# Two transformer blocks in split fp32 on one core: GpSimd makes no weights' low parts after the attention in the latent mixers

## The chip, the core and the metric

One core of a Trainium2 chip. The time is the device time of one execution in microseconds, median of the runs. TensorE (PE) multiplies; the vector engine (DVE), ScalarE (ACT) and GpSimd (POOL) work beside it, each through its own list of instructions in order; SyncE (SP) issues the transfers.

## What is computed

The program runs two blocks one after the other; the change lies in the first, which has two layers. Each layer mixes 512 latent tokens (and, in layer 0, 256 context tokens) of width 1024. The mixer, cut to what matters here:

```
def merge_branches(z, attn_o, ...):
    conv_o = conformer_conv(z[..., V_END:CONV_END], ...)   # depthwise conv of 31 taps, layer norm, silu, 1024x1024 product
    pool_o = multiscale_pool(z[..., CONV_END:POOL_END], pool_w, pool_scale)
    gates = jax.nn.sigmoid(z[..., POOL_END:].reshape(z.shape[:-1] + (N_BRANCH, D_MODEL)))
    m = gates[..., 0, :] * attn_o + gates[..., 1, :] * conv_o + gates[..., 2, :] * pool_o
    return m @ w_out + b_out
```

with z = h @ w_in + b_in, everything in float32.

## The kernel before

A product in float32 is made from three matmuls of halves (L181 to L183): each operand is kept as a high part (a rounded copy) and a low part (the value minus the high part). Weights come in units of 1024 rows by 128 columns (512 KB). `Net.unit` fetches one into one of three `raw` buffers (SyncE, L167), ScalarE casts the high part (L152), and then the low part is made (L153, `tensor_sub`), on the vector engine or on GpSimd. A counter decides:

```
on_pool = self.units * self.pool_share % 12 < self.pool_share
```

For the whole mixer `pool_share` is 6 in the latent streams, so that every second unit's low part is GpSimd's; before the mixer and behind its pointwise product it is 0. A `raw` buffer is free for the next fetch when its low part is made.

A latent mixer runs in this order. First the attention, between whose steps the first channel blocks of the depthwise convolution are started. Then `rest()`: what is left of the convolution's products, the pooling branch, and the gates of attention (`gate0`, `between`) and pooling. Then `conv_ln`, woven with the convolution's gate (`gate1`); then `pointwise`; then the output product.

Who does what there:
- the convolution: eight channel blocks, each a chain of 30 taps on the vector engine (L830, one instruction per tap of 128x512). `chain_work` releases taps between the other steps.
- the pooling branch (`pooled`): L902 copies a product into `pad` (ScalarE); L914 adds shifted copies, L918 multiplies, L919 subtracts (GpSimd); the result is cast (ScalarE, L152) and its low part made (vector engine, L153). `mixed` multiplies it (L936, L937 on the vector engine).
- `gate0`: L877 (ScalarE), L882 (GpSimd), L883 (vector engine), eight times.
- `conv_ln`: L964 transposes the eight blocks on TensorE for their moments, a matmul each spreads mean and scale over the partitions (R[0] and R[1], L977 and L979); then per block L983 (GpSimd), L984 (vector engine), L986 and L987 (ScalarE), L988 (vector engine) and a split.
- layer 0 also carries, as `extra`, the products that make the next modulation vectors (L499 to L509): they take units of another weight, L504 copies the row on ScalarE and L506 multiplies it.

A tiling framework schedules the instructions, so the order on each engine follows from its own estimates and isn't that of the text. PSUM has three buffers for products, named mm.

Of the kernel before, what the change touches and what calls it, by code (L numbers as in the profile page):

```python
# [1679 lines left out]
def run(*gens):  # L1680
    for g in gens:
        for _ in g:
            pass


def weave(*gens):

    live = [list(g) for g in gens]
    while live:
        for e in list(live):  # L1690
            e.append(0) if len(e) == 2 else None
            e[2] += e[1]
            while e[2] >= 1:
                e[2] -= 1
                if next(e[0], "end") == "end":
                    live.remove(e)
                    break


def first_block(net, stop=None):  # L1700
    nc, A = net.nc, net.A
    lat, cx = Stream("lat", 0, LAT), Stream("ctx", 1, CTX)
# [5 lines left out]
    def chain_work(chains, n):  # L1708

        if net.mark is None:  # L1710
            return
        with net.tc.issue_after(net.mark.ins):
            while n > 0 and chains:
                for c in list(chains[:2]):
                    if next(c, "end") == "end":
                        chains.remove(c)
                    n -= 1

    def mix(l, S, X, kT, vs, nkeys, rope, bc_mod, xin, xout, h_out, before_out=None, extra=None):

        od = net.dram([P, KD, S.T])
        m = net.chunked(S.T)
        convh = net.chunked(S.T)
        chains, chains2 = [], []
        conv = net.conv_gemm(l, S, X, convh, chains, chains2)
        with net.tc.issue_after(net.mark.ins) if net.mark else nullcontext():
            for _ in range(FRONT[S.nt]):
                next(conv)

        def gap():  # L1730
            for _ in range(GAP[S.nt]):
                if len(chains) < net.BUFS["pad"]:
                    with net.tc.issue_after(net.pe_mark.ins):
                        next(conv, None)

        def attn():
            for kv in range(2):
                qt = {}

                def dst(t, qt=qt):  # L1740
                    if t // 2 not in qt:
                        qt[t // 2] = net.sb([P, 2, 2, 4, P], F32R, "s8")
                    return qt[t // 2][:, t % 2]

                yield from net.q_half(l, X, kv, rope, dst)
                yield from net.attend(S.nt, dst, kT[kv], lambda kc, kv=kv: vs(kc, kv), nkeys,
                                      lambda t, h, kv=kv: od[:, 4 * kv + h : 4 * kv + h + 2, t * P : t * P + P],
                                      lambda t, h, kv=kv: sums[:, t, 4 * kv + h : 4 * kv + h + 1], gap)

        n = 0  # L1750
        net.mark = net.pe_mark = None
        sums = net.sb([P, S.nt, 8], F32, "sums")
        net.pool_share = SHARE[S.nt]
        for _ in attn():
            n += 1
            chain_work(chains, RATE[S.nt])
            chain_work(chains2, 5)
            if extra is not None and n % EXTRA[S.nt] == 0:
                next(extra, None)
        sig = net.chunked(S.T)  # L1760
        rows = net.inverse_rows(sums, S.nt)
        bout = net.bias_rows([A["b_out"][l, 512 * i : 512 * i + 512] for i in range(2)], 2.0)

        def rest():
            yield from conv
            yield from net.pool_branch(l, S, X, m, net.gate0(l, S, X, m, od, lambda: rows))

        for n, _ in enumerate(rest()):
            chain_work(chains, 10)
            chain_work(chains2, 3)  # L1770
            if extra is not None and n % REXT[S.nt][0] == REXT[S.nt][1]:
                next(extra, None)
        if extra is not None:
            run(extra)
        chain_work(chains, 1000)
        chain_work(chains2, 1000)
        C = Feat(net, S.T, KD)
        if X.full is not None:
            C.full = convh
        weave((net.conv_ln(l, S, convh, C), 1.5), (net.gate1(l, S, X, sig), 1))  # L1780
        M = Feat(net, S.T, KD)
        bc = net.ln_prep(A["ln1_g"][l], A["ln1_b"][l], bc_mod, net.gate_row(l, S.s, 0))
        run(net.pointwise(l, S, C, sig, m, M))
        net.pool_share = 0
        if before_out is not None:
            before_out()
        run(net.out_ln(S, M, A["w_out"][l], bout, bc, xin, xout, h_out))
# [60 lines left out]
    with net.tc.issue_after(net.pe_mark.ins):  # L1848
        net.load_cols(0)
    Xl = []  # L1850
    mix(0, cx, Xc, kT, lambda kc, kv: V(kc)[:, kv * P : kv * P + P], CTX, False,
        None, c0, xd["ctx", 0], None,
        before_out=lambda: Xl.append(net.first_h(lat, x0, 0)), extra=net.ada(0, 4, 6))
# [4 lines left out]
    Xcf = []  # L1858
    Xf = Feat(net, LAT, KD)
    mix(0, lat, Xl, kT, vs, LAT + CTX, True, net.mod_rows(0, 0, 1), x0, xd["lat", 0], h_feat(Xf),  # L1860
        before_out=lambda: Xcf.append(reload(cx, xd["ctx", 0], net.mod_rows(0, 1, 1))), extra=net.ada(0, 6, 12))
    if stop == "mix0":
# [12 lines left out]
    vs = lat_keys(1, X1, kT, V, Xc1)  # L1875
    Xf = Feat(net, LAT, KD)
    mix(1, lat, X1, kT, vs, LAT + CTX, True, net.mod_rows(1, 0, 1), xd["lat", 1], xd["lat", 2], h_feat(Xf))
    if stop == "mix1":
        return xd["lat", 2], None
# [112 lines left out]
```

## Time and profile before

| | us |
|---|---|
| median of 3 runs | 3969.94 (3968.89 to 3973.01) |
| profiled execution | 3973.06 |
| its span, first to last instruction | 3971.3 |
| TensorE busy | 3743.3 (94%), mean granted clock 0.973 |
| vector engine busy | 2541.1 (64%) |
| ScalarE busy | 1438.2 (36%) |
| GpSimd busy | 904.4 (23%) |

Busy times are sums over the span. In square brackets behind an instruction of a timeline stands how long its engine was idle before it, and which instruction released it. A tile's name is its tag; the number behind it, where one is given, says which tile of that tag it is.

### The profile page before, as it was taken

To read this page: it belongs to the slowest core of one execution; us is meant where nothing else is said; L and a number is where in the kernel's file an instruction comes from. 1 tells how busy PE (TensorE), PEld (TensorE's weight loads), DVE (VectorE), ACT (ScalarE), POOL (GpSimd) and SP (SyncE) were. 2 spreads that over 40 slices of the span, in tenths; PEclk is the share of its full clock that TensorE was granted. 3 is DMA by queue.
4 is the path that set the end of the run, shared out by engine and by line. 5 is a ranking of instruction groups with operands and counts; after the bars stand their busy time and mean duration, and the time that the engine had idled before them with its cause. 6 is when DMAs were issued, how large, how long until landed. Compare 5 with 4: busy or idle time off the path is not lost. (4 is left out here: it accounts for less than half of the span.)

```text
span 3971.3 us, 48183 instructions
## 1 busy us (share of the span) xinstructions
PE 3743.3 (94%) x18265; PEld 3098.8 (78%) x18265; DVE 2541.1 (64%) x3600; ACT 1438.2 (36%) x2608; POOL 904.4 (23%) x978
## 2 busy tenths in 40 slices
PE   7899998799899999899989899999899999999999
PEld 3688886577688888688767788889788888778887
DVE  2987888967876656878886645563454346764444
ACT  1535443334222222344324233234432235643223
POOL 0441423673200002522554200110000002420000
PEclk8999999899899999899999999999999999999999
DMA  5567223454343333222333423333233332033332
GB/s 189 144 166 220 88 63 90 118 150 156 110 143 117 123 117 103 79 72 62 103 96 120 132 85 117 106 123 99 84 98 95 97 102 65 17 96 96 96 101 90
DMA packets 491474, 429.49 MB, mean 108 GB/s; under 512 B 29590, under 2 KB 389630, under 8 KB 491242
## 3 DMA queue, kind: packets, MB, share of 16 engines
q1 hardware_dynamic: 491162, 426.16, 35.2%
q8 instruction: 143, 2.34, 0.2%
q14 instruction: 89, 0.73, 0.1%
q0 software_dynamic: 80, 0.26, 0.0%
HBM read 404.70 MB, written 21.65 MB: 107 GB/s over the span
## 5 line engine op out<-in xcount | busy, mean ns | idle before, releaser
L181 PE MATMUL mm<-s,w 128*128 128x512 f32 (+2 forms) x2840 | 1044.3, 370 | 37.1 <-ACT t L877 9.5
L182 PE MATMUL mm<-s,w 128*128 128x512 f32 (+2 forms) x2840 | 1040.8, 367 | 13.5 <-DVE s L153 13.5
L183 PE MATMUL mm<-s,w 128*128 128x512 f32 (+2 forms) x2840 | 1037.7, 366 | 0.0
L152 ACT CAST w<-raw 128x1024 fp32r<-128x1024 f32 (+3 forms) x570 | 582.4, 1026 | 769.7 <-PE mm L183 429.6
L153 DVE TENSOR_TENSOR w<-raw,w 128x1024 fp32r<-128x1024 f32 (+3 forms) x484 | 628.8, 1302 | 273.4 <-ACT w L152 268.3
L181 PE MATMUL mm<-w,s 128*128 128x512 f32 (+2 forms) x1928 | 735.8, 382 | 8.9 <-DVE t L1098 3.7
L182 PE MATMUL mm<-w,s 128*128 128x512 f32 (+2 forms) x1928 | 728.2, 378 | 1.3 <-DVE w L153 1.3
L183 PE MATMUL mm<-w,s 128*128 128x512 f32 (+2 forms) x1928 | 726.6, 379 | 0.8 <-DVE s L153 0.8
L181 PEld LDWEIGHTS mm<-s,w 128*128 128x128 f32 (+1 forms) x2840 | 539.2, 191 | 137.5 <-ACT t L877 10.3
L182 PEld LDWEIGHTS mm<-s,w 128*128 128x128 f32 (+1 forms) x2840 | 541.2, 191 | 100.5 <-DVE s L153 16.3
L183 PEld LDWEIGHTS mm<-s,w 128*128 128x128 f32 (+1 forms) x2840 | 540.6, 190 | 86.5 <-issue 0.2
L830 DVE SCALAR_TENSOR_TENSOR s<-pad,cols,s 128x512 f32<-128x512 f32 (+1 forms) x690 | 523.4, 811 | 1.7
L181 PEld LDWEIGHTS mm<-w,s 128*128 128x128 f32 x1928 | 364.2, 189 | 85.0 <-issue 7.3
L182 PEld LDWEIGHTS mm<-w,s 128*128 128x128 f32 x1928 | 364.3, 189 | 64.4 <-DVE w L153 2.2
L183 PEld LDWEIGHTS mm<-w,s 128*128 128x128 f32 x1928 | 363.9, 189 | 63.8 <-DVE s L153 1.6
L360 POOL TENSOR_SCALAR st<-st 128x1 f32<-128x1 f32 (+2 forms) x91 | 32.2, 354 | 1269.3 <-ACT s L1217 900.2
L153 POOL TENSOR_TENSOR w<-raw,w 128x1024 fp32r<-128x1024 f32 (+1 forms) x86 | 244.2, 2842 | 286.3 <-ACT w L152 276.0
L152 ACT CAST s<-b 128x256 fp32r<-128x256 f32 (+2 forms) x224 | 104.5, 474 | 176.6 <-DVE s L153 90.6
L1232 DVE TENSOR_TENSOR s<-s,mm 128x512 f32<-128x512 f32 x80 | 54.6, 685 | 172.0 <-PE mm L183 172.0
L1054 POOL MEMSET pad<- 128x1 f32 x66 | 6.4, 99 | 650.0 <-DVE t L1061 648.8
L153 DVE TENSOR_TENSOR s<-b,s 128x256 fp32r<-128x256 f32 (+2 forms) x224 | 119.7, 545 | 43.8 <-ACT s L152 42.6
L1248 DVE TENSOR_TENSOR t<-t 128x512 f32<-128x512 f32 x64 | 44.2, 691 | 153.3 <-ACT t L1247 153.3
(297 smaller groups left out, 4423.8 us busy)
## 6 DMA issues: line engine op xcount, KB each, us to landing
raw<-in_w_up SPq DMA_DIRECT2D x152, 512.0 KB
raw<-in_w_in SPq DMA_DIRECT2D x147, 512.0 KB
raw<-in_w_down SPq DMA_DIRECT2D x108, 512.0 KB
w<-in_w_ada SPq DMA_DIRECT2D x48, 512.0 KB
w<-in_w_in SPq DMA_DIRECT2D x33, 512.0 KB
raw<-in_w_ada SPq DMA_DIRECT2D x32, 512.0 KB
raw<-in_w_out SPq DMA_DIRECT2D x24, 512.0 KB
t<-d SPq DMA_DIRECT2D x44, 256.0 KB
```

Source lines behind the costliest of these rows:

```text
L152: self.nc.scalar.copy(hi, src)
L153: (eng or self.nc.vector).tensor_sub(lo, src, hi.bitcast(F32))
L181: mm(out, lhsT=l[0], rhs=r[0], start=first, stop=False)
L182: mm(out, lhsT=l[0], rhs=r[1], start=False, stop=False)
L183: return mm(out, lhsT=l[1], rhs=r[0], start=False, stop=last)
L360: nc.gpsimd.tensor_scalar(out, src, scalar1=scale, scalar2=eps, op0=ALU.mult, op1=ALU.add)
L830: nc.vector.scalar_tensor_tensor(out=o, in0=pad[:, k : k + T], scalar=self.col("dww", 8 * k + j), in1=o, op0=ALU.mult, op1=ALU.add)
L1054: nc.gpsimd.memset(pad[:, 0:1], 0.0)
L1232: nc.vector.tensor_add(x(t)[:, cs], x(t)[:, cs], ps)
L1248: nc.vector.tensor_mul(r, r, r)
```

## The change

The counter is set to 0 for the latent streams as soon as the attention loop has ended, not only behind the pointwise product:

```
@@ -1757,6 +1757,8 @@
             chain_work(chains2, 5)
             if extra is not None and n % EXTRA[S.nt] == 0:
                 next(extra, None)
+        if S is lat:
+            net.pool_share = 0
         sig = net.chunked(S.T)
         rows = net.inverse_rows(sums, S.nt)
         bout = net.bias_rows([A["b_out"][l, 512 * i : 512 * i + 512] for i in range(2)], 2.0)
```

56 low parts go from GpSimd to the vector engine, 34 in layer 0 and 22 in layer 1; 52 are of 128x1024, four of 128x512. GpSimd's low parts in the context mixer, in the attentions and in the second block stay. The scheduler orders the engines' lists anew around it.

On the vector engine in layer 0, w_5974 and w_5979 are units of the modulation product mm_5982, w_6009 is the pooling weight; s_862 are the convolution's blocks 4 to 7, whose taps read pad_4702, pad_4891 and pad_5081. Before:

```order
L153 TENSOR_TENSOR w_5974<-raw_5972,w_5974 128x1024
L153 TENSOR_TENSOR s_972_5685<-pad_5736,s_972_5685 128x512
L830 SCALAR_TENSOR_TENSOR s_862_5043<-pad_5081,cols_301,s_862_5043 128x512
L830 SCALAR_TENSOR_TENSOR s_862_5043<-pad_4891,cols_301,s_862_5043 128x512
L830 SCALAR_TENSOR_TENSOR s_862_5043<-pad_5081,cols_301,s_862_5043 128x512
L883 SCALAR_TENSOR_TENSOR s_996_5833<-t_1000_5875,s_1001_5877 128x512
L830 SCALAR_TENSOR_TENSOR s_862_5043<-pad_4891,cols_301,s_862_5043 128x512
L830 SCALAR_TENSOR_TENSOR s_862_5043<-pad_5081,cols_301,s_862_5043 128x512
L830 SCALAR_TENSOR_TENSOR s_862_5043<-pad_4891,cols_301,s_862_5043 128x512
```

and the list of the change at the same place:

```order
L153 TENSOR_TENSOR s_972_5685<-pad_5736,s_972_5685 128x512
L830 SCALAR_TENSOR_TENSOR s_862_5043<-pad_4702,cols_301,s_862_5043 128x512
L153 TENSOR_TENSOR w_5974<-raw_5972,w_5974 128x1024
L830 SCALAR_TENSOR_TENSOR s_862_5043<-pad_5081,cols_301,s_862_5043 128x512
L830 SCALAR_TENSOR_TENSOR s_862_5043<-pad_4891,cols_301,s_862_5043 128x512
L883 SCALAR_TENSOR_TENSOR s_996_5833<-t_1000_5875,s_1001_5877 128x512
L830 SCALAR_TENSOR_TENSOR s_862_5043<-pad_4702,cols_301,s_862_5043 128x512
L153 TENSOR_TENSOR w_5979<-raw_5977,w_5979 128x1024
L830 SCALAR_TENSOR_TENSOR s_862_5043<-pad_5081,cols_301,s_862_5043 128x512
```

GpSimd's splits (here w_5979) now lie between the taps, and the taps stand later: from the unit w_5516 to w_6009's split there were 67 taps and 9 weight splits on the vector engine, and there are 53 and 18; pad_4702's chain, done before this place in the old list, is still running. In layer 1, from the unit w_15197 to the first L936 of mixed (t_2364), there were 73 taps, 5 large splits and one of 128x512, and there are 64, 10 and two.

On GpSimd at the start of the pooling branch in layer 0 (pad_5340 is its first sum, the s tiles of L882 belong to gate0):

```order
-L153 TENSOR_TENSOR w_5511<-raw_5509,w_5511 128x1024
 L914 TENSOR_TENSOR pad_5340<-pad_5336 128x512
 L882 TENSOR_TENSOR s_937_5441<-s_937_5441 128x512
+L882 TENSOR_TENSOR s_943_5489<-s_943_5489 128x512
 L918 TENSOR_TENSOR pad_5340<-pad_5340,t_923_5334 128x512
-L882 TENSOR_TENSOR s_943_5489<-s_943_5489 128x512
 L882 TENSOR_TENSOR s_959_5581<-s_959_5581 128x512
 L882 TENSOR_TENSOR s_964_5628<-s_964_5628 128x512
-L919 TENSOR_TENSOR pad_5340<-pad_5340,pad_5336 128x512
 L882 TENSOR_TENSOR s_995_5829<-s_995_5829 128x512
 L882 TENSOR_TENSOR s_1001_5877<-s_1001_5877 128x512
-L153 TENSOR_TENSOR w_5521<-raw_5519,w_5521 128x1024
```

L919 comes behind these last two L882 now; it is the same in layer 1.

On TensorE in layer 0 the transposes of block 5 of the convolution stood right behind those of block 4, ahead of mm_5793; in the changed list they stand behind the product mm_5982:

```order
-L964 MATMUL b_1150_6690<-ident_66,s_862_5043 128x128
-L964 MATMUL b_1156_6736<-ident_66,s_862_5043 128x128
 L506 MATMUL mm_5793<-ar_5789,sel_102 2x512
 L181 MATMUL mm_5802<-s_495_2806,w_5799 128x512
...
 L499 MATMUL mm_5982<-w_5974,cw_97 4x512 x4
 L499 MATMUL mm_5982<-w_5979,cw_97 4x512 x4
+L964 MATMUL b_1150_6690<-ident_66,s_862_5043 128x128
+L964 MATMUL b_1156_6736<-ident_66,s_862_5043 128x128
 L506 MATMUL mm_6003<-ar_5999,sel_102 2x512
```

The pair moved by one modulation product, with the pairs of blocks 6 and 7 moving later in the same way; the matmul of R[1] stands one product later as well. On ScalarE in layer 1 the activation L877 of mm_15357 now stands ahead of the cast of pad_15288, which it followed.

## Rows read from the trace of the kernel before

**Rows 1.** The page's busy us of each engine, share of the span, instructions.

```profile
PE 3743.3 (94%) x18265; PEld 3098.8 (78%) x18265; DVE 2541.1 (64%) x3600; ACT 1438.2 (36%) x2608; POOL 904.4 (23%) x978
```

**Rows 2.** Timeline of TensorE, layer 0: start, us, operation, idle before and its releaser.

```profile
682.44 2.11 PE L499 MATMUL mm<-w,cw 128*4 128x512 f32 x5 [4.95 <-ACT pad L902]
...
697.06 1.86 PE L506 MATMUL mm<-ar,sel 32*2 32x512 f32 x2 [9.19 <-ACT ar L504]
...
740.17 0.69 PE L964 MATMUL b<-ident,s 128*128 128x128 f32 x2 [11.33 <-DVE s L830]
...
742.58 0.79 PE L181 MATMUL mm<-s,w 128*128 128x512 f32 x1
...
747.44 0.45 PE L183 MATMUL mm<-s,w 128*128 128x512 f32 x1
...
749.82 0.39 PE L181 MATMUL mm<-s,w 128*128 128x512 f32 x1
...
776.58 1.86 PE L506 MATMUL mm<-ar,sel 32*2 32x512 f32 x2 [5.89 <-ACT ar L504]
...
930.27 0.50 PE L182 MATMUL mm<-s,w 128*128 128x512 f32 x1 [1.67 <-DVE s L153]
```

**Rows 3.** Timeline of TensorE, layer 1.

```profile
1949.35 0.80 PE L181 MATMUL mm<-s,w 128*128 128x512 f32 x1 [4.93 <-ACT pad L902]
...
2003.63 0.80 PE L181 MATMUL mm<-s,w 128*128 128x512 f32 x1 [9.00 <-ACT t L877]
...
2027.89 0.80 PE L181 MATMUL mm<-s,w 128*128 128x512 f32 x1 [8.78 <-DVE t L936]
...
2140.10 0.74 PE L181 MATMUL mm<-s,w 128*128 128x512 f32 x1 [4.75 <-ACT s L867]
```

**Rows 4.** Windows: busy us (instructions) of PE, PEld, DVE, ACT, POOL; clock.

```profile
664.50:770.40 105.90, 78.77 (x306) 54.34 (x304) 87.27 (x90) 30.10 (x37) 83.57 (x42) 0.85 0.40 115
...
800.00:900.00 100.00, 97.28 (x418) 71.75 (x417) 57.99 (x49) 38.15 (x48) 79.56 (x68) 0.98 0.52 149
```

**Rows 5.** Timeline of the vector engine and of ScalarE before 776.58.

```profile
770.42 0.68 DVE L153 TENSOR_TENSOR w<-raw,w 128x512 fp32r<-128x512 f32 x1
...
775.95 0.57 ACT L504 COPY ar<-mm 4x512 f32<-4x512 f32 x1
```

**Rows 6.** Groups of the vector engine in both stretches: busy us, mean ns.

```profile
L830 DVE SCALAR_TENSOR_TENSOR s<-pad,cols,s 128x512 f32<-128x512 f32 x68 | 63.6, 987 | 0.0
...
L153 DVE TENSOR_TENSOR w<-raw,w 128x1024 fp32r<-128x1024 f32 x9 | 14.7, 1638 | 8.0 <-ACT w L152 8.0
...
L830 DVE SCALAR_TENSOR_TENSOR s<-pad,cols,s 128x512 f32<-128x512 f32 x74 | 73.2, 1046 | 0.0
```

**Rows 7.** Timeline of the vector engine, three rows, and of GpSimd.

```profile
710.30 1.21 DVE L153 TENSOR_TENSOR w<-raw,w 128x1024 fp32r<-128x1024 f32 x1
...
717.75 5.37 DVE L830 SCALAR_TENSOR_TENSOR s<-pad,cols,s 128x512 f32<-128x512 f32 x8
...
742.15 3.38 DVE L153 TENSOR_TENSOR w<-raw,w 128x1024 fp32r<-128x1024 f32 x1
...
741.64 2.81 POOL L153 TENSOR_TENSOR w<-raw,w 128x1024 fp32r<-128x1024 f32 x1
```

**Rows 8.** Groups of GpSimd: weight splits in layer 0, then in layer 1.

```profile
L153 POOL TENSOR_TENSOR w<-raw,w 128x1024 fp32r<-128x1024 f32 x10 | 40.9, 4101 | 7.0 <-ACT w L152 7.0
...
L153 POOL TENSOR_TENSOR w<-raw,w 128x1024 fp32r<-128x1024 f32 (+1 forms) x7 | 21.4, 3053 | 19.1 <-ACT w L152 17.9 <-DVE s L830 1.2
```

**Rows 9.** Timeline of GpSimd, start of the stretch in layer 0.

```profile
662.02 11.93 POOL L914 TENSOR_TENSOR pad<-pad 128x512 f32<-128x512 f32 x1 [24.59 <-DVE s L830]
...
679.89 1.26 POOL L919 TENSOR_TENSOR pad<-pad,pad 128x512 f32<-128x512 f32 x1
```

**Rows 10.** Timeline of GpSimd and of ScalarE ahead of 2140.10.

```profile
2130.92 6.13 POOL L153 TENSOR_TENSOR w<-raw,w 128x1024 fp32r<-128x1024 f32 x2
...
2138.84 0.62 ACT L152 CAST s<-s 128x512 fp32r<-128x512 f32 x1 [5.15 <-DVE s L988]
```

More of the change, by code (lines that the diff above doesn't have):

```diff
@@ L1759, in mix @@
                 next(extra, None)
+        if S is lat:
+            net.pool_share = 0
         sig = net.chunked(S.T)
```

## The prediction

> **What bounds the kernel now.** I read the page first: TensorE is busy 94% of the span, the vector engine 64%, GpSimd 23% [rows 1]. An engine at 94% sets the end, and what is to be won is its waits and the stretches in which its clock is low. So the views in order were: the page, the table of windows, the waits of TensorE in the two stretches that the change touches, and then, at each wait, the engine that released it.
>
> The change acts from the end of the attention to the end of the pointwise product of the two latent mixers: about 660 to 965 us in layer 0, about 1915 to 2170 us in layer 1. The longest waits of TensorE there stand in [rows 2] and [rows 3]: 4.95, 9.19, 11.33 and 5.89 us in layer 0 and 1.67 us at its end, 4.93, 9.00, 8.78 and 4.75 us in layer 1. After a long wait the clock is at its lower level for a while: from 742.58 to 747.44 eleven matmuls take 4.86 us, from 747.44 to 749.82 ten take 2.38 us [rows 2], so the eleven cost 2.2 us more than they would at the upper level. From 800 to 900 us TensorE is busy 97.28 us and the vector engine only 57.99 [rows 4]; there nothing is to be won on TensorE.
>
> Who stands behind the waits? The 5.89 us at 776.58 is a copy on ScalarE (L504, at 775.95). It follows a cast whose weights could only be fetched when the vector engine had made the low part of w_6009, at 770.42 [rows 5]; three `raw` buffers go round. The 11.33 us names the vector engine's convolution taps (L830) outright, the 8.78 us its L936. The reader is to see that both stretches are set by how fast the vector engine gets through its list, in order: to w_6009's split in layer 0, to L936 in layer 1.
>
> **What the vector engine does there.** From 664.5 to 770.4 us, 105.9 us, it is busy 87.27 us [rows 4]: 68 taps of mean 987 ns and 9 weight splits of mean 1638 ns are most of it; from 1931.4 to 2027.1 us 74 taps of mean 1046 ns [rows 6]. Undisturbed, eight taps take 5.37 us, 0.67 each, and a 128x1024 split takes 1.21 us [rows 7]. So the taps are held back 68 x (0.987 - 0.67) = 21.6 us and the splits 9 x (1.638 - 1.21) = 3.9 us in layer 0, 25.5 us together, and 74 x (1.046 - 0.67) = 27.8 us for the taps in layer 1. What holds them is seen at 742.15: a split that takes 3.38 us in place of 1.21 while GpSimd makes its own split, 741.64 to 744.45 [rows 7]. One meeting costs the vector engine 2.17 us.
>
> **The change part by part.** 56 low parts move, 34 in layer 0 and 22 in layer 1; 52 have 128x1024 elements and four 128x512. At 1.21 us (half that for the four) it is 65 us more of work on the vector engine, 41 of them in layer 0. In layer 0 most of this lies where the vector engine has room (58% at 800 to 900 us). In the critical stretches the order absorbs it: up to w_6009's split the vector engine's list had 67 taps and 9 splits, and has 53 taps and 18 splits. Own time: 67 x 0.67 + 9 x 1.21 = 55.8 us before, 53 x 0.67 + 18 x 1.21 = 57.3 us now, +1.5 us. Fourteen taps were put off. To L936 in layer 1 it was 73 taps and 5 large splits and is 64 and 10: 55.0 us before, 55.0 now, and one 128x512 split more, +0.6.
>
> What is won is the holding. GpSimd makes 10 splits in the first stretch, mean 4101 ns, and 7 in the second, mean 3053 ns [rows 8]. The bounds: nothing, if the 22 short additions and products that GpSimd still has in each stretch fill the room and each now holds a tap; or all ten (seven) meetings, 10 x 2.17 = 21.7 us and 7 x 2.17 = 15.2 us. I choose between: some of the 10 fell into the 18.6 us in which the vector engine idled, and a mean of 4101 ns, where 2.81 us was a disturbed one already [rows 7], says that some were kept waiting themselves and held nobody most of that time. I take 60%: -13 us in layer 0 and -9 us in layer 1. This choice carries the forecast.
>
> Added on the way is the beginning of each stretch. The first addition of the pooling branch takes 11.93 us at 662.02, since the vector engine works without a gap beside it, and its end L919 comes at 679.89 [rows 9]. A ScalarE cast waits for L919, L902 stands behind that cast, and TensorE waits for L902 (4.95 us). Now two more L882 stand ahead of L919. An instruction of their size takes GpSimd 1.26 us (L919's own row), so L919 comes 2.5 us later at least; and the vector engine, which then lay idle, has a few taps to do beside them. I take +4 us for the vector engine's own wait (it needs the same cast), bounds +2.5 and +8.
>
> Here the Trainium skill speaks against the change. Its page "SBUF — State Buffer", section "SBUF: two separate sides", says that VectorE and GpSimd share one pair of ports under an exclusive lock for a whole instruction, and that a VectorE operation with two SBUF inputs takes it too. By that a split on the vector engine shuts out GpSimd's pooling chain just as the reverse does; the 3.38 us and the 11.93 us agree. By the rule alone three moved splits ahead of L919 would put it off by 3 x 1.21 = 3.6 us more in each layer, and the sum below would be 7 us less gain.
>
> **The sum.** Layer 0: the vector engine reaches w_6009's split 13 - 1.5 - 4 = 7.5 us earlier, and the wait at 776.58 ends so much earlier; the 11.33 us wait before it goes, because the second pair of transposes moves behind mm_5982, but TensorE then waits longer for the same copy, so it isn't counted again. One stretch of low clock goes with it: -2. At the end something is given back. The matmul that spreads R[1] stands one product later in TensorE's list (24 matmuls of 0.24 us, 5.7 us by the pitch of [rows 2]), and the normalised convolution follows it to the pointwise product, where the wait is 1.67 us now. GpSimd's splits no longer lie in that chain. I take +4 (bounds 0 and +10). Layer 0: -7.5 - 2 + 4 = -5.5 us. Layer 1: -9 + 0.6 + 4 = -4.4 us at L936; the cast that stood ahead of the L877 of the 9.00 us wait is now behind it, which saves one clock stretch, -2; and the 4.75 us at 2140.10, a ScalarE activation queued behind a cast that waited 5.15 us for the vector engine while GpSimd did two splits in 6.13 us [rows 10], shrinks by 3. Layer 1: -9.4 us. Together -15 us: 3973.06 us of the profiled execution becomes 3958. Its span is 3971.3 us and 1.8 us lie around it; it is 3.1 us over the median of the three runs, 3969.94, against which the forecast is 3955 us.
>
> **The rivals.** A measurement of this kernel can tell about 0.2%, 8 us, from no change.
> 1. *Forecast*, 8 to 26 us gained (3944 to 3962): chance 0.46.
> 2. *The gain is larger.* All seventeen meetings counted (-36.9 instead of -22) and nothing given back at the pointwise product: -15 - 15 - 4 = -34, 3936 us. For it: every tap of [rows 6] is a third to a half over its undisturbed time. Against: 22 short GpSimd instructions per stretch stay, and they hold taps too. Chance 0.12.
> 3. *No change that can be told.* GpSimd's remaining chain runs closer to the taps, half of the 22 us is held by it (+11), and L919 is late by the upper bound in one layer (+4): 3970 us. For it: TensorE's first wait in both layers comes from that chain, not from a split. Chance 0.23.
> 4. *Slower.* The vector engine is the bound and stays as held as it was: the short instructions, no longer spaced by splits, each meet a tap. Then own work counts (+1.5, +0.6), L919 at its upper bound (+8 twice), and the chain to the pointwise product at +10; nothing comes off but 2 + 3 + 2 us: +21, 3991 us; with half of these 3980. It decides from the point at which less than 6 of the 22 us of holding go. For it: 87.27 of the 105.9 us are busy already [rows 4] and 41 us more come to the layer. Against: the list to w_6009 is no longer than it was. Chance 0.19.
>
> **How the numbers follow.** The likeliest case gives 3955 us. Rival 2 ends at 3936 and rival 4 begins near 3978; leaving out about one in ten on either side gives 3934 to 3977, which takes in the bounds of the holding and of L919; the likeliest case's own range is 3944 to 3962. Faster by over 0.2% is the forecast and rival 2, 0.58; the same 0.23; slower 0.19.
>
> **What would show it.** In the profile after: taps from the attention's end to w_6009's split of mean near 0.8 us in place of 0.987; no transpose waiting 11 us near 740; the matmul after w_5979 that waits for L504 started 8 us earlier than 776.58; L936 some 4 us before 2027.16, counted from the same start; a first wait (for L902) longer than 4.95 and 4.93; a wait at the pointwise product longer than 1.67. The forecast is wrong if the mean of the taps stays above 0.93 us, or if L919 comes more than 8 us later, or if the pointwise product of layer 0 waits over 10 us.

## The result, and the profile after

The changed kernel takes 3931.95 us (3931.53 to 3932.28, 4 runs) against 3971.48 us before (3968.89 to 3974.59, 4 runs). The ratio is 0.9897, 95% interval [0.9883, 0.9912]: 39.5 us faster, where 15 were forecast. The time lies below the stated range. Its profiled execution takes 3932.28 us.

The page's busy time of the kernel after, as [rows 1]:

```profile
PE 3731.6 (95%) x18265; PEld 3091.5 (79%) x18265; DVE 2534.9 (64%) x3656; ACT 1438.8 (37%) x2608; POOL 754.3 (19%) x922
```

The vector engine makes 56 low parts more, and is busy 6.2 us less. What it was given is less than what it was held up by.

TensorE's timeline after, to be read against [rows 2] and [rows 3] (start, us, idle before and its releaser):

```profile
673.65 1.55 PE L499 MATMUL mm<-w,cw 128*4 128x512 f32 x6
...
687.87 1.86 PE L506 MATMUL mm<-ar,sel 32*2 32x512 f32 x2 [10.36 <-ACT ar L504]
...
754.73 1.01 PE L506 MATMUL mm<-ar,sel 32*2 32x512 f32 x2 [0.49 <-ACT ar L504]
...
791.63 0.80 PE L183 MATMUL mm<-s,w 128*128 128x512 f32 x1 [4.30 <-DVE w L153]
...
1929.52 0.79 PE L181 MATMUL mm<-s,w 128*128 128x512 f32 x1 [4.69 <-ACT pad L902]
...
1989.93 0.79 PE L181 MATMUL mm<-s,w 128*128 128x512 f32 x1 [6.93 <-DVE t L936]
...
2105.52 0.50 PE L181 MATMUL mm<-s,w 128*128 128x512 f32 x1 [1.19 <-ACT s L867]
```

The same matmuls, before and after: the product mm_5524 began at 682.44 behind a wait of 4.95 us and begins at 673.65 behind none; the L506 of 697.06 now comes at 687.87, that of 776.58 at 754.73, 21.9 us earlier. In layer 1 the product that waited for L936 until 2027.89 starts at 1989.93, 38.0 us earlier, and the one that waited for L867 until 2140.10 starts at 2105.52. So TensorE leads by 21.9 us in the middle of layer 0, by 24.5 at the end of layer 1's attention, by 38.0 at its L936 and by 40.8 at the end of the span. New, smaller waits show where some was given back: 4.30 us for a weight split of the vector engine at 791.63.

Not all of this was won in the stretches that the prediction looked at. The weights of the moved units are fetched ahead, so in each layer three of GpSimd's moved splits ran while the attention was still going on. The first of layer 0 met two taps (0.67 us each when undisturbed), and TensorE waited behind them; the rows are of before, the last one of after:

```profile
586.47 2.55 POOL L153 TENSOR_TENSOR w<-raw,w 128x1024 fp32r<-128x1024 f32 x1 [2.64 <-ACT w L152]
586.69 3.54 DVE L830 SCALAR_TENSOR_TENSOR s<-pad,cols,s 128x512 f32<-128x512 f32 x2
...
599.67 4.44 PE L766 MATMUL acc<-s,s 128*128 128x256 f32 x12 [2.47 <-DVE s L153]
```

```profile
598.09 2.86 PE L766 MATMUL acc<-s,s 128*128 128x256 f32 x12 [0.35 <-DVE s L153]
```

The wait is shorter by 2.1 us and the twelve matmuls by 1.6, and TensorE reaches the end of layer 0's attention with a lead of 3.7 us. The same step of 4 us comes in the runs e1 and e3 below, which move these splits too, and not in e2 and e4, which don't.

The vector engine's groups after (busy us, mean ns, idle before), from the split of w_949 (659.4) to that of w_6009 (746.2) in layer 0, and from the split at 1905.0 to L936 (1989.2) in layer 1, as [rows 6]:

```profile
L830 DVE SCALAR_TENSOR_TENSOR s<-pad,cols,s 128x512 f32<-128x512 f32 x54 | 43.7, 844 | 0.0
L153 DVE TENSOR_TENSOR w<-raw,w 128x1024 fp32r<-128x1024 f32 x18 | 25.5, 1417 | 3.7 <-ACT w L152 3.7
...
L830 DVE SCALAR_TENSOR_TENSOR s<-pad,cols,s 128x512 f32<-128x512 f32 x65 | 55.7, 905 | 0.0
```

and the windows of the first of these stretches and of 800 to 900 us, as [rows 4]:

```profile
659.40:746.20 86.80, 70.12 (x277) 50.88 (x276) 75.78 (x85) 27.12 (x34) 51.06 (x32) 0.86 0.48 147
800.00:900.00 100.00, 99.61 (x440) 76.75 (x439) 66.71 (x75) 45.50 (x59) 40.54 (x43) 1.00 0.48 143
```

The stretch takes 86.8 us in place of 105.9, that of layer 1 84.2 in place of 95.7. The mean tap fell from 987 to 844 ns and from 1046 to 905 ns; the vector engine's idle time in the first fell from 18.6 to 11.0 us (105.90 less 87.27 busy, 86.80 less 75.78). From 800 to 900 us it is busy 8.7 us longer, and TensorE runs through.

### The profile page after: what moved, and what is told of

Same layout as the page of the kernel before. It is cut to its first block, busy times and chain, and to the rows that moved or that the text cites. A ratio compares the mean times of both kernels' runs of the same rounds, so it can differ in the third digit from the quotient of the medians.

```text
span 3930.5 us, 48189 instructions
## 1 busy us (share of the span) xinstructions
PE 3731.6 (95%) x18265; PEld 3091.5 (79%) x18265; DVE 2534.9 (64%) x3656; ACT 1438.8 (37%) x2608; POOL 754.3 (19%) x922
## 5 line engine op out<-in xcount | busy, mean ns | idle before, releaser
L153 DVE TENSOR_TENSOR w<-raw,w 128x1024 fp32r<-128x1024 f32 (+2 forms) x540 | 686.0, 1274 | 266.0 <-ACT w L152 261.4
L181 PEld LDWEIGHTS mm<-s,w 128*128 128x128 f32 (+1 forms) x2840 | 538.4, 190 | 124.9 <-DVE t L936 13.1
L182 PEld LDWEIGHTS mm<-s,w 128*128 128x128 f32 (+1 forms) x2840 | 540.5, 190 | 97.5 <-DVE s L153 13.1
L830 DVE SCALAR_TENSOR_TENSOR s<-pad,cols,s 128x512 f32<-128x512 f32 (+1 forms) x690 | 494.5, 766 | 1.5
L914 POOL TENSOR_TENSOR pad<-pad 128x512 f32<-128x512 f32 (+13 forms) x60 | 103.8, 1729 | 221.4 <-ACT pad L902 150.9
```

Of the source, the lines that this page charges most:

```text
L153: (eng or self.nc.vector).tensor_sub(lo, src, hi.bitcast(F32))
L181: mm(out, lhsT=l[0], rhs=r[0], start=first, stop=False)
L182: mm(out, lhsT=l[0], rhs=r[1], start=False, stop=False)
L830: nc.vector.scalar_tensor_tensor(out=o, in0=pad[:, k : k + T], scalar=self.col("dww", 8 * k + j), in1=o, op0=ALU.mult, op1=ALU.add)
L914: nc.gpsimd.tensor_add(nxt[:, a:b], cur[:, a + s0 : b + s0], cur[:, a + s1 : b + s1])
```

## The experiments

Two theories stood against each other. *Holding*: a split on GpSimd keeps the vector engine's instructions waiting while both run, and the vector engine's list sets TensorE's pace. *Lateness*: GpSimd's splits come late themselves, behind other work in its list, so that TensorE and the three raw buffers wait for them. Every run was compared with runs of the kernel before on the same chip.

**Where it is won.** The change in one layer, then in one half of the mixer:

```diff
e1   if S is lat and l == 0: net.pool_share = 0
e2   if S is lat and l == 1: net.pool_share = 0
e3   as the change; ahead of weave(conv_ln, gate1): net.pool_share = SHARE[S.nt]
e4   as before; ahead of weave(conv_ln, gate1): if S is lat: net.pool_share = 0
```

> The change in layer 0 alone (layer 1 as before). If the two stretches act each on their own, TensorE's lead of 24.5 us at the end of layer 0 in the trace after stays and nothing else comes: 24 us faster than before, 3947 us. If the lead of layer 1 (15 us more) hangs on that of layer 0, more than 30 us; if it was given back later, less than 15.

> The change in layer 1 alone. If the stretches act on their own: 15 us faster than before, 3957 us, with L936 of t_2364 some 13 us earlier against the start of the mixer. If the result needs layer 0: within 5 us of before.

> GpSimd splits no weights from the end of the attention to conv_ln, and again every second one from conv_ln on. If the gain is made where the convolution's taps run: 33 to 39 us faster, 3933 to 3938 us. If it is made at conv_ln and the pointwise product (GpSimd's splits among L983 and L868): under 10 us.

> The other half: GpSimd splits as before up to conv_ln and none from there to the end of the pointwise product. If the gain is made where the taps run: 0 to 5 us faster (the 4.75 us wait at 2140.10 and the 1.67 us one at 930.27), 3966 to 3971 us. If at conv_ln: 25 us or more.

e1: 3951.81 us against 3976.3, ratio 0.9941 [0.9926, 0.9955], 24 us faster. e2: 3960.82 us, 0.9962 [0.9947, 0.9977], 15 us. They add to the whole, as expected: each layer acts on its own. e3: 3946.0 us, 0.9923 [0.9908, 0.9938], 31 us by the ratio, short of the 33 to 39 expected; e4: 3961.87 us, 0.9968 [0.9955, 0.998], 13 us. So some three quarters lie where the taps run, and conv_ln to the pointwise product has more than the 0 to 5 us that I expected. In e4's trace the wait for L867, [rows 3], is nearly gone; it starts at 2129.78:

```profile
2129.78 0.50 PE L181 MATMUL mm<-s,w 128*128 128x512 f32 x1 [1.20 <-ACT s L867]
```

That accounts for somewhat over a quarter of its 13 us; where the rest lies the trace doesn't settle, since 4.7 us of its lead of 11.6 stand there at 591 us, long before its lists differ from those of before. By so much two executions can differ. e3 and e4 together make 44 us by their ratios, where the change makes 41.

**What it is.** In e5 the vector engine makes all low parts as in the change, and GpSimd takes the same 56 differences over again, into the raw buffer, for nobody. In e6 it only writes zeros there:

```diff
 # Net.unit, behind the split; the condition that picks the 56 units is left out here
e5 +  self.nc.gpsimd.tensor_sub(raw[:rows, :n], raw[:rows, :n], w[:rows, 0, :n].bitcast(F32))
e6 +  self.nc.gpsimd.memset(raw[:rows, :n], 0.0)
```

> The changed kernel, in which GpSimd besides takes the same differences as before the change, of the same 56 units, into the raw buffer (nobody reads them; the vector engine's low parts are used). If GpSimd's splits cost by holding the vector engine (2.2 us at a meeting): most of the 39.5 us is lost again, 25 us or more over the changed kernel, and the mean of the taps between w_949 and w_6009 goes back to 0.95 us or more. If they cost because the low parts themselves came late to TensorE: within 10 us of the changed kernel, since the low parts are the vector engine's here.

> As e5_redo, but GpSimd only writes zeros over the raw buffer of those 56 units: the buffer stays with GpSimd's queue as it did before, and GpSimd reads nothing. If the holding is what costs: within 10 us of the changed kernel. If the late release of raw buffers by GpSimd's queue is what costs: 20 us or more over it.

e5: 3999.1 us against 3974.49, ratio 1.0062 [1.0047, 1.0077]: the whole gain is lost, and 25 us more, 67 us over the changed kernel. e6: 3931.78 us, 0.9896 [0.9878, 0.9914]: the same as the changed kernel. The busy times of e5, then of e6:

```profile
PE 3746.5 (94%) x18265; PEld 3100.1 (78%) x18265; DVE 2622.6 (66%) x3656; ACT 1439.1 (36%) x2608; POOL 921.8 (23%) x978
...
PE 3726.5 (95%) x18265; PEld 3090.3 (79%) x18265; DVE 2533.0 (64%) x3656; ACT 1439.9 (37%) x2608; POOL 797.0 (20%) x978
```

The vector engine has the same 3656 instructions in both and in the changed kernel. It is busy 87.7 us longer in e5 than in the changed kernel, and 1.9 us less in e6. That the zeros are shorter doesn't explain this: GpSimd is busy 167.5 us longer in e5 and 42.7 in e6, and at e5's rate e6 would have cost the vector engine some 22 us (an estimate). The groups of e5 in the stretch that answers to 659.4 to 746.2 (its taps, its weight splits, GpSimd's repeated differences, and the window), then the same of e6:

```profile
L830 DVE SCALAR_TENSOR_TENSOR s<-pad,cols,s 128x512 f32<-128x512 f32 x56 | 59.0, 1096 | 0.0
L153 DVE TENSOR_TENSOR w<-raw,w 128x1024 fp32r<-128x1024 f32 x18 | 27.0, 1498 | 7.4 <-ACT w L152 7.4
...
L173 POOL TENSOR_TENSOR raw<-raw,w 128x1024 f32<-128x1024 f32 x9 | 33.7, 3745 | 18.4 <-DVE w L153 18.4
...
659.50:767.80 108.30, 78.23 (x311) 55.43 (x309) 94.45 (x87) 29.04 (x36) 79.58 (x41) 0.84 0.39 115
```

```profile
L830 DVE SCALAR_TENSOR_TENSOR s<-pad,cols,s 128x512 f32<-128x512 f32 x54 | 47.1, 909 | 0.0
...
L173 POOL MEMSET raw<- 128x1024 f32 x9 | 8.6, 955 | 12.1 <-DVE w L153 12.1
...
659.70:747.00 87.30, 69.72 (x290) 51.50 (x289) 76.54 (x85) 27.63 (x34) 55.78 (x41) 0.88 0.47 140
```

With the differences on GpSimd the stretch takes 108.3 us, with the zeros 87.3, and in the changed kernel 86.8. The low parts that TensorE uses are the vector engine's in all three, so low parts that come late from GpSimd can't be the reason; and in e6 GpSimd's list holds the raw buffers as well, for a short instruction. The holding is seen directly in e5, on the vector engine (three taps, 5.48 us where 0.67 each is usual) and on GpSimd beside it:

```profile
745.89 5.48 DVE L830 SCALAR_TENSOR_TENSOR s<-pad,cols,s 128x512 f32<-128x512 f32 x3
...
746.37 2.75 POOL L173 TENSOR_TENSOR raw<-raw,w 128x1024 f32<-128x1024 f32 x1
```

e5 keeps a raw buffer longer than e6 does (3.7 us in place of 1.0), and what that costs isn't told apart by a run of its own. The stretch bounds it: of the 21.5 us by which it is longer than in the changed kernel, 18.7 are busy time of the vector engine (94.45 against 75.78), and its waits for the casts of weights grew by 3.7 us (from 3.7 to 7.4).

**By how much.** One unit in four on GpSimd, in place of one in two:

```diff
-            net.pool_share = 0
+            net.pool_share = 3
```

> Every fourth unit's low part on GpSimd after the attention, in place of every second (before) and none (after). If each split that is taken away brings the same: half of the gain, 20 us faster than before. If the gain hangs on single places of the order (ScalarE's list at the start of each mixer): near either before or after.

e8: 3951.94 us, 0.9943 [0.9928, 0.9958], 23 us faster than before: a little over half. So the gain doesn't hang on one place in the order; whether it is even from split to split, one point between can't tell.

**What is left on GpSimd.** gate0's products L882 on the vector engine too, with the change (e7) and without it (e9); conv_ln's L983 as well (e11):

```diff
-            nc.gpsimd.tensor_mul(o, o, inv)
+            (nc.vector if S.nt == 4 else nc.gpsimd).tensor_mul(o, o, inv)
e11, besides:
-            nc.gpsimd.tensor_mul(h, h, R[:, 0, :T])
+            (nc.vector if nt == 4 else nc.gpsimd).tensor_mul(h, h, R[:, 0, :T])
```

> The changed kernel with gate0's eight products L882 on the vector engine too, in the latent mixers. If the wait for L504 at 687 us (10.36 us in the profile after) comes from GpSimd's chain of L914, L882 and L919, it shrinks by the six L882 ahead of L919, some 9 us, in both layers together 5 to 15 us faster than the changed kernel. If the vector engine is the bound there, 16 products of 0.7 us make it up to 11 us slower.

> The kernel before (GpSimd splits every second unit) with only gate0's L882 on the vector engine in the latent mixers. If what holds the vector engine is any GpSimd instruction that meets it, sixteen products fewer on GpSimd help here as in e7: 8 to 15 us faster than before. If they only matter once the splits are gone (the first cast then is the last thing that TensorE waits for): within 5 us of before.

> As e7_l882_vector, with conv_ln's eight products L983 on the vector engine too in the latent mixers. If GpSimd's L983 still hold L984 and the splits there: 2 to 6 us faster than e7 (3919 us). If TensorE has nothing left to wait for in conv_ln: the same as e7 within 3 us.

e7: 3919.34 us, 0.9862 [0.9848, 0.9877]; this interval lies below that of the change, so it beats both kernels, by some 13 us and by 55. But the wait that I named shrinks by 3 us only, from 10.36 to 7.39:

```profile
684.90 1.86 PE L506 MATMUL mm<-ar,sel 32*2 32x512 f32 x2 [7.39 <-ACT ar L504]
```

More comes from the vector engine, whose stretch takes 77.1 us in place of 86.8, with seven products more in it, and five taps and one split of the pooling branch fewer (the window of e7 from w_949 to w_6009):

```profile
663.90:741.00 77.10, 68.99 (x286) 49.27 (x285) 69.92 (x87) 26.86 (x34) 24.99 (x19) 0.93 0.50 153
```

Over the whole run the vector engine is busy 2535.0 us in e7, against 2534.9 in the changed kernel, with sixteen products of 0.68 us more: some 11 us of holding went, which fits short two-operand instructions of GpSimd holding it too.

e9: 3956.42 us, 0.9954 [0.994, 0.9969], 18 us faster than before, more than expected. That it is less holding, as I expected, the trace doesn't bear out. In the stretch of layer 0 (662.0 to 758.2) the taps are held more than before, 1119 ns in place of 987; what went is the vector engine's idle time, 2.1 us in place of 18.6:

```profile
L830 DVE SCALAR_TENSOR_TENSOR s<-pad,cols,s 128x512 f32<-128x512 f32 x68 | 72.9, 1119 | 0.0
...
662.00:758.20 96.20, 76.75 (x306) 54.38 (x304) 94.08 (x92) 29.76 (x37) 53.85 (x34) 0.89 0.44 128
```

With L882 out of GpSimd's list, its chain from the first L914 to the end of L919 is 7.7 us in place of 19.1, and the vector engine doesn't wait for the cast behind it. So beside the holding there is a lateness, not of GpSimd's splits but of its short chain. What it is worth isn't settled: in layer 1 the chain is as short, but TensorE's lead grows there by 1 us only, against 14 in layer 0.

e11: 3918.79 us, 0.9859 [0.9844, 0.9873], not to be told from e7.

**In the attention.** No low parts on GpSimd in the latent mixers at all (e10), and with e7 (e12):

```diff
-        net.pool_share = SHARE[S.nt]
+        net.pool_share = 0 if S is lat else SHARE[S.nt]
```

> The changed kernel, with no low parts on GpSimd in the attention of the latent mixers either (20 more move). The vector engine carries the softmax and taps there. If the holding costs there as well: 5 to 15 us faster than the changed kernel. If the vector engine is so full in the attention that the splits' own 1.21 us count: up to 15 us slower.

> e7 and e10 together. If their gains are of different stretches they add: the sum of the two against the changed kernel. If both clear the same start of the pooling branch: no more than the better of the two.

e10: 3926.36 us, 0.9878 [0.9863, 0.9893]; its interval overlaps that of the change, [0.9883, 0.9912], so 6 to 8 us better are likely and not shown. e12: 3916.1 us, 0.9858 [0.9842, 0.9874], not to be told from e7: the two gains don't show as a sum. The version to take is e7; e11 and e12 add nothing that can be told.

## Why the prediction was wrong

The direction was right, and the holding, which carried the forecast, came nearly as it was priced; the size was too small by 24.5 us. What failed is the vector engine's idle time, which was to grow at the beginning of each stretch and shrank, and the reach of the change, which was put too late. Point by point:

1. *The holding*, -13 and -9 us at my 60%. In layer 0 the taps were held 54 x (0.844 - 0.67) = 9.4 us after and the 18 splits 18 x (1.417 - 1.21) = 3.7 us, 13.1 together against 25.5 before: -12.4, as forecast. In layer 1 the taps were held 65 x (0.905 - 0.67) = 15.3 us against 27.8: -12.5 where I took -9. e5 shows that such differences on GpSimd hold it. Missed: 3.5 us.
2. *Own work*, +1.5 us: 54 taps and 18 splits make 58.0 us against 68 and 9 with 56.5. Right.
3. *The beginning of each stretch*, +4 us "for the vector engine's own wait (it needs the same cast)": the step that failed. L919 did come later: from the start of the first L914 to its end it is 24.4 us, and was 19.1 in [rows 9]. The rows of GpSimd after, then of the vector engine before and after:

```profile
658.34 12.34 POOL L914 TENSOR_TENSOR pad<-pad 128x512 f32<-128x512 f32 x1 [39.65 <-DVE s L830]
...
681.45 1.26 POOL L919 TENSOR_TENSOR pad<-pad,pad 128x512 f32<-128x512 f32 x1
```

```profile
681.84 1.09 DVE L153 TENSOR_TENSOR s<-pad,s 128x512 fp32r<-128x512 f32 x1 [8.79 <-ACT s L152]
```

```profile
660.61 4.05 DVE L830 SCALAR_TENSOR_TENSOR s<-pad,cols,s 128x512 f32<-128x512 f32 x6
...
665.72 4.06 DVE L830 SCALAR_TENSOR_TENSOR s<-pad,cols,s 128x512 f32<-128x512 f32 x6
671.96 1.77 DVE L883 SCALAR_TENSOR_TENSOR s<-t,s 128x512 f32<-128x512 f32 x1 [2.18 <-POOL s L882]
...
683.40 1.31 DVE L153 TENSOR_TENSOR s<-pad,s 128x512 fp32r<-128x512 f32 x1 [4.25 <-ACT s L152]
```

   The vector engine no longer lies idle until that cast: its new list puts an L883, taps and a weight split ahead, and it waits 2.18 and 4.25 us there, 6.4 together in place of 8.8: -2.4 where I wrote +4. In layer 1 its idle time was 8.8 us of the 95.7 (95.7 less 86.90 busy), all of it before such casts, and is 6.4 of the 84.2: again -2.4. That is 12.8 us. The rest of the fall in layer 0, from 18.6 to 11.0 us over the stretch, is 5.2 us that the sum had no term for, most of it shorter waits for the casts of weights (8.0 us in [rows 6], 3.7 after); what brought those casts forward isn't shown. And TensorE's first wait, which I had longer in both layers, went in layer 0 and is 4.69 us after 4.93 in layer 1. In layer 0 an L877 stands ahead of the cast in ScalarE's new list. That it frees the buffer for mm_5524 is argued from the order and from that product's start, 673.65, without a wait; no run shows it alone.
4. *Where the change begins*, "about 660" and "about 1915 us": it began with the splits from 586.47 on, and the lead of 3.7 us that TensorE brings into layer 0's stretch has no term in the sum. In layer 1, where the first moved split ran at 1855, it gains 1.3 us before the stretch.
5. *The lock.* The Trainium skill ("SBUF — State Buffer", "SBUF: two separate sides") describes an exclusive lock between the two engines that is held for a whole instruction. By that the prediction made L919 later still and the gain 7 us smaller. The trace agrees that L919 came later, by 5.3 us; the 7 us didn't come, since the vector engine waits less for its cast than before.
6. *Given back at the pointwise product*, +4: nothing was; the 1.67 us wait is gone as well. About as much, 4.30 us, was given back earlier, at 791.63.
7. *The 4.75 us wait for L867*, -3: it is 1.19 us, -3.6. Right, and e4 shows it with GpSimd's splits taken from that part alone.

These points can't be added up to the 24.5 us, since what the vector engine wins TensorE doesn't always keep. TensorE's lead in the two profiled executions, 40.8 us where 15 were forecast, tells where the miss of 25.8 lies. Layer 0 brought 22.1 us (3.7 of them ahead of the stretch) where 5.5 were forecast; layer 1, from the end of its attention to the end of its mixer, 11.6 where 9.4 were. Another 2.4 us came between the two, 1.3 of them by point 4, and 4.7 behind layer 1's mixer, where the change moves no low part. The lead of e3 falls by 4 us in that last part, so the 4.7 aren't to be told from the difference between two executions. So most of the miss is layer 0's: points 3, 4 and 6.

Of the rivals, the second, "the gain is larger", at 0.12, came nearest in size (3936 us), but only half for its reason: nothing was given back at the pointwise product, while the holding that went is 24.9 us in the two stretches and not its 36.9. The rest of the agreement is luck. None of the three signs by which the forecast was to be known as wrong came true; they all watched for less gain. I gave the fourth rival 0.19. In e5 the vector engine has all splits and stays held, as in that rival, and the kernel is 25 us slower than before, where I had worked out 21; but there it is repeated differences that hold it, and not short instructions, so the closeness of the numbers says little.

## What to carry to other kernels

An instruction that is given to an idle engine isn't free if it holds those of a busy one: here a GpSimd split of 2.81 us cost the vector engine some 2.2 us at a meeting, more than the 1.21 us that it needs for the same work. Not every one meets: over all 56, e5's repeated differences cost 1.6 us each (87.7 us of busy time), which is still more. Compare the mean of the busy engine's instructions with their shortest time in the stretch, before sharing its work out. And when a list is ordered anew, read for each engine what stands ahead of an instruction that waits, not only when its input comes.

## What the runs showed of the hardware

- GpSimd's differences of two operands hold the vector engine (tap mean 1096 ns in e5, 87.7 us more busy time in all). Zeros written by GpSimd for the same units don't, over the whole run (1.9 us less busy time, the same device time), though in the stretch of layer 0 the tap mean is 909 ns, against 844 without them. For a vector engine operation with two inputs in SBUF, the Trainium skill ("SBUF — State Buffer", "SBUF: two separate sides") restricts the lock to a GpSimd operation that reads SBUF; e5 and e6 agree.
- Who waits isn't always the same engine. Beside a gapless run of taps a GpSimd addition of 128x512 took 12.34 us (11.93 before), where L919 of the same size takes 1.26; the vector engine was not slowed meanwhile (six taps in 4.06 us), and the addition ended at 670.68, 0.9 us after the vector engine had paused. At 742.15 in [rows 7] it was the vector engine that waited, for a split that GpSimd had begun 0.5 us earlier.
